# Contributions of seven chunks to the mLSTM states, formed beside the convolution units of the second half

## The chip, the cores and the metric

One core of one Trainium2 chip runs the whole program. The metric is device time in microseconds (us) for one execution. The engines are TensorE (PE), VectorE (DVE), ScalarE (ACT), GpSimd (POOL) and SyncE (SP). Each has its own queue of instructions and goes through it in order, and an instruction waits until what it needs is there. SP and ACT also issue the DMAs.

## What is computed

A transformer block over 2048 rows of width 1024: a norm, one input projection, a pooling mixer and a bidirectional mLSTM scan beside it, an output projection, and a gated MLP. Cut to what matters here:

```python
def mlstm_bidir(q, k, v, gates, st_f, st_b):      # forward scan, and one over the flipped rows
    ...
c_new = decay[..., None, None] * c0 + jnp.einsum('bhs,bhsv,bhsd->bhvd', wk, vc, kc)
n_new = decay[..., None] * n0 + jnp.einsum('bhs,bhsd->bhd', wk, kc)
...
hx_m, _, _ = mlstm_bidir(qx, kx, vx, gx, st_f, st_b)
...
mix_x = jnp.concatenate([pool_x, mlstm_output(hx_m, ox, head_norm[l])], axis=-1) @ w_out[l]
x = x + g1 * mix_x
x = x + g2 * swiglu(modulate(rmsnorm(x, norm2[l]), sh2, sc2), w_up[l], w_down[l])
```

The einsum over the rows of a chunk (weighted keys times values) needs no state. Only the scan, decay times old state plus this contribution, goes from chunk to chunk.

## The kernel before

The sequence is cut into 16 chunks of 128 rows (NCH = 16), the context into 2. The input projection runs in two halves of 1024 rows and by units of two times 128 columns. One unit is seven products of 12 matmuls with 512 columns each (`product`, three matmuls of split operands for each of four k); `unit` numbers them by their operands, A[0] to A[6], and takes them in the order 0, 1, 4, 3, 5, 2, 6. The operands A[0] and A[1] may take buffers named "vt" (four of them, in the pool `vtp`), the others "wh" and "wl".

In the second half come two pool units, the k unit and the q unit (`conv_unit`: after its products each row goes through three steps of the short convolution, a silu, and a store to `s_k` or `s_q`, the "y" instructions at L471 to L474), and then two o units whose products are interleaved. Beside the o units runs `chunk_step`, called in the middle and at the end of each of their products, 18 times in all for 2 context and 16 sequence chunks:

- `load_ahead` and `dma_kv` (L897, L899) load a chunk's keys and values from DRAM on SP;
- `delta_a` turns the keys (two PE transposes, L945) and scales them with the gates (VectorE, L948);
- `delta_b` multiplies with the values (four PE matmuls, L958, eight rows in the profile) and ScalarE copies the result into the state tiles (four copies, L963), which `ST(k)` finds in three tiles, h0, h1 and h5;
- `scan_step` (four VectorE operations, L968) adds decay times the state before. It is called only when both directions' contributions of a step are there, which the order 0, 15, 1, 14, ... gives.

With the o units done, the remaining `chunk_step`s follow one behind another. Then `load_wo` loads the output projection's weights (in small tiles L988 and in big ones L984), scales them (L990, L993) and splits them (L148, L151); its first parts are called among the steps. Then a loop over the chunks: `ml_a` (scores L1090, exponentials L1097, L1099), `ml_b` (L1114, L1120, reciprocal L1125 to L1127, heads L1131 to L1134, L1136), `prep` (transposes L1155), `proj` (L1171 to L1173). The MLP follows.

The order in which each engine meets its instructions is not the order of the code: a scheduler of the framework, with its own model of durations, places them, and an `issue_after` in the code adds an edge to it. The exponentials of all chunks but the first, and the loads of `prep`, have such an edge behind the last copies of the state contributions:

```python
with tc.issue_after(last_act[0].ins), tc.issue_after((copies[-1] if n else last_act[0]).ins):
    for d in range(2):
        for h in range(4):
            nc.scalar.activation(X[:, d, h, :], X[:, d, h, :], AF.Exp, bias=tokq[:, 0, d, h, cc:cc + 1])
```

Of the kernel before, what the change touches and what calls it, by code (L numbers as in the profile page):

```python
# [8 lines left out]
F32 = mybir.dt.float32  # L9
# [12 lines left out]
def tile_hybrid_block(ctx: ExitStack, tc: tile.TileContext, x, c, cx, c_ctx, w_ada, b_ada, norm1, w_in, conv_qk,  # L22
                      gate_bias, pool_w, pool_scale, head_norm, w_out, norm2, w_up, w_down, norm_f, out):
    nc = tc.nc
# [101 lines left out]
    s_g = dram.tile([4, D], F32, name="s_g")  # L126
    s_w = dram.tile([6, 4, 2, P, 512], F32, name="s_w")
    s_e = dram.tile([NCH // 2, P, 512], F32, name="s_e")

# [563 lines left out]
    def run_units(units, psp, wp, tmp, fetch, bg=None):  # L695


        for n, (srcs, sink, after, w, half) in enumerate(units):
            if half:
                make = operands(load_raws(srcs, kept=True), [wp], kept=s_w[w])  # L700
            else:
                make = operands(load_raws(srcs), [wp], keep_=s_w[w])
            A = {}
            for j, i in enumerate(ORDER):
                A[i] = make(i)
                if n == 0 and Btile[j] is None:
                    fetch(j)
            for j, _ in enumerate(unit(A, psp, tmp, sink)):
                if bg and (n, j) in bg:
                    bg.pop((n, j))()  # L710
            after()
# [15 lines left out]
    def conv_unit(bp, half, i0):  # L727
        pre = [bp.tile([P, TH + 3], F32, name=f"pre{r}") for r in range(2)]
        for r in range(2):
            if half == 0:  # L730
                nc.gpsimd.memset(pre[r][:, 1:2], 0.0)
            else:
                nc.gpsimd.tensor_copy(pre[r][:, 0:2], edge[:, i0 + r])
                nc.gpsimd.memset(pre[r][:, TH + 2:TH + 3], 0.0)

        def sink(r, n, ps, sb):
            o = pre[r][:, 2 + n * 512:2 + (n + 1) * 512]
            if sb is None:
                nc.scalar.copy(o, ps)
            else:  # L740
                nc.vector.tensor_tensor(o, ps, sb, op=ALU.add)

        def after():
            for r in (0, 1):
                i = i0 + r
                rows = (s_q, s_k)[i // 2][i % 2 * P:(i % 2 + 1) * P]
                y = bp.tile([P, TH + 1], F32, name="y", bufs=2)
                if half == 0:
                    nc.gpsimd.tensor_copy(edge[:, i], pre[r][:, TH:TH + 2])
                    n, o, t0 = TH - 1, 1, 0  # L750
                else:
                    n, o, t0 = TH + 1, 0, TH - 1
                conv_silu(y[:, :n], pre[r][:, o:], n, conv_w(i), y[:, :n])
                nc.sync.dma_start(rows[:, t0:t0 + n], y[:, :n])
        return in_cols(O_Q + i0 * P), sink, after, i0 // 2, half
# [70 lines left out]
    def o_unit(tmp, half, i0):  # L826
# [8 lines left out]
            nc.scalar.dma_start(s_so[i * P:(i + 1) * P, b * 512:(b + 1) * 512], so)  # L835
        return in_cols(O_O + i0 * P), sink, lambda: None, 4 + i0 // 2, half

    for half in range(2):
        if half:
            Btile = [None] * 7  # L840
# [39 lines left out]
        else:  # L880
# [1 line left out]
            plp.close()  # L882
            rxp = pf.enter_context(pool("rx", 1, "right"))
            with pool("cvp", 1) as bp:
                run_units([conv_unit(bp, half, i0) for i0 in (2, 0)], pu_, wp, tmp, fetch, {(0, 3): fin})
            padr.close()
    tpp.close()

# [17 lines left out]
    bp = pj.enter_context(pool("pja", 1))  # L906
    tmps = (tmp, bp)

    seq = [(True, cc) for cc in range(NCC)] + [(False, cc) for i in range(NCH // 2) for cc in (i, NCH - 1 - i)]
    todo_kv, loaded = list(seq), []  # L910

    def load_ahead():
        if todo_kv:
            is_ctx, cc = todo_kv.pop(0)
            src = (s_kc, s_vc) if is_ctx else (s_k, s_v)
            kp = bp if not is_ctx and len(todo_kv) < 12 and len(todo_kv) % 4 < 2 else kvp
            loaded.append(dma_kv(kp, *src, cc, 2, kvp if is_ctx or cc in (0, NCH - 1) else None))

    for _ in range(2):
        load_ahead()  # L920
# [645 lines left out]
```

## Time and profile before

| | us |
|---|---|
| median of three runs | 2118.39 |
| runs | 2116.07 to 2119.63 |
| profiled execution, its time | 2117.76 |
| its span, first to last instruction | 2115.9 |
| PE busy | 2015.6 (95% of the span) |
| mean granted clock of PE | 0.982 |

The profile is of one execution; 1.9 us of its time lie outside the span. A row of a timeline begins with its start and its length, and ends with the idle time ahead of it and what ended that. "x8" puts equal neighbours together. A DMA's row is its issue, not its landing.

### The profile page before, as it was taken

The page shows a single profiled execution, that of the slowest core. Times are in us where ns is not written, and L with a number is a line of the kernel's source. Part 1 is how long each engine was busy: PE and PEld are TensorE (multiplying, and loading weights), DVE is VectorE, ACT ScalarE, POOL GpSimd, SP SyncE. Part 2 cuts the span into 40 slices and gives each one's busy share as a digit, 9 for nine tenths or more (in the row PEclk, how much of TensorE's full clock was granted, in tenths as well). Part 3 has the DMA queues.
Part 4 walks back from the last instruction along what each step waited for, and adds up shares of the span by engine and source line. Part 5 has one row for each costly group of instructions (what it writes and reads, how often), then busy time and mean ns, then how long its engine had stood idle before and what let it go on. Part 6 is the DMA issues. An engine that isn't in the chain of part 4 may idle for free.

```text
span 2115.9 us, 27589 instructions
## 1 busy us (share of the span) xinstructions
PE 2015.6 (95%) x9482; PEld 1637.0 (77%) x9482; DVE 1365.8 (65%) x2333; ACT 899.1 (42%) x1787; POOL 227.0 (11%) x222
## 2 busy tenths in 40 slices
PE   7999989996999998999999999999999999999998
PEld 3997757775777776788888877888888788888887
DVE  6866868757455566666675588677677554447664
ACT  6643644456444444433333354333333343433442
POOL 1000013211333320000000000000000002004121
PEclk9999999997999999999999999999999999999999
DMA  8598989689586756433342367555565584644642
GB/s 281 169 297 270 301 269 329 219 262 254 138 253 209 241 184 183 140 124 125 100 159 85 100 217 256 189 194 189 174 199 192 190 309 149 226 139 168 226 158 100
DMA packets 365812, 421.42 MB, mean 199 GB/s; under 512 B 23924, under 2 KB 241624, under 8 KB 364904
## 3 DMA queue, kind: packets, MB, share of 16 engines
q1 hardware_dynamic: 319728, 348.22, 50.9%
q10 hardware_dynamic: 45944, 71.43, 10.5%
q8 instruction: 75, 1.23, 0.2%
q14 instruction: 65, 0.53, 0.1%
HBM read 280.45 MB, written 139.12 MB: 198 GB/s over the span
## 4 chain that ended last, share of the span: by engine, by line
PE 74%; DMA 11%; DVE 5%; ACT 4%; issue 3%; SPq 1%; POOL 1%; ACTq 0%; DVEq 0%; POOLq 0%
PE pa L642 8%; PE pa L644 8%; PE pa L643 8%; PE pdn L1392 7%; PE pdn L1393 7%; PE pdn L1394 7%; PE pg L642 4%; PE pg L643 4%; PE pg L644 4%; PE pb L642 2%; PE pb L644 2%; PE pb L643 2%; PE pm L1171 2%; PE pm L1173 2%; PE pm L1172 2%
## 5 line engine op out<-in xcount | busy, mean ns | idle before, releaser
L642 PE MATMUL pa<-h,wh 128*128 128x512 f32 x680 | 271.0, 400 | 7.6 <-ACT p L656 4.7
L644 PE MATMUL pa<-h,wl 128*128 128x512 f32 x680 | 269.8, 397 | 0.3 <-DMA wl<-s_w 0.3
L643 PE MATMUL pa<-h,wh 128*128 128x512 f32 x680 | 269.5, 397 | 0.0
L148 ACT CAST wh<-ws 128x512 fp32r<-128x512 f32 x200 | 123.5, 619 | 281.3 <-PE pg L643 154.2
L1392 PE MATMUL pdn<-ow,op 128*128 128x512 f32 x616 | 236.8, 389 | 1.0 <-ACT op L148 1.0
L1393 PE MATMUL pdn<-ow,op 128*128 128x512 f32 x616 | 237.5, 389 | 0.0
L1394 PE MATMUL pdn<-ow,op 128*128 128x512 f32 x616 | 237.5, 389 | 0.0
L151 DVE TENSOR_TENSOR op<-ra,op 128x512 fp32r<-128x512 f32 x154 | 121.6, 796 | 159.4 <-ACT op L148 159.3
L148 ACT CAST op<-ra 128x512 fp32r<-128x512 f32 x154 | 95.2, 621 | 225.9 <-PE pdn L1394 223.9
L642 PE MATMUL pg<-h,wh 128*128 128x512 f32 x448 | 177.8, 397 | 2.9 <-ACT h L148 1.7
L643 PE MATMUL pg<-h,wh 128*128 128x512 f32 x448 | 178.6, 399 | 0.9 <-DVE h L151 0.8
L644 PE MATMUL pg<-h,wl 128*128 128x512 f32 x448 | 177.5, 396 | 0.0
L151 DVE TENSOR_TENSOR wl<-ws,wh 128x512 fp32r<-128x512 f32 x200 | 136.4, 685 | 55.4 <-ACT wh L148 55.2
L642 PEld LDWEIGHTS pa<-h,wh 128*128 128x128 f32 x680 | 129.0, 190 | 43.2 <-ACT p L656 6.0
L644 PEld LDWEIGHTS pa<-h,wl 128*128 128x128 f32 x680 | 128.5, 189 | 31.1 <-issue 0.5
L643 PEld LDWEIGHTS pa<-h,wh 128*128 128x128 f32 x680 | 128.8, 189 | 30.2 <-issue 1.0
L1424 POOL TENSOR_TENSOR hr<-hr,o 128x1024 f32<-128x1024 f32 x8 | 21.7, 2734 | 1096.7 <-ACT o L1437 927.0
L1392 PEld LDWEIGHTS pdn<-ow,op 128*128 128x128 f32 x616 | 115.6, 188 | 25.5 <-ACT op L148 1.4
L1393 PEld LDWEIGHTS pdn<-ow,op 128*128 128x128 f32 x616 | 115.7, 188 | 23.9
L1394 PEld LDWEIGHTS pdn<-ow,op 128*128 128x128 f32 x616 | 115.7, 188 | 23.9
L613 DVE TENSOR_TENSOR ws<-raw 128x512 f32<-128x512 f32 x100 | 69.0, 690 | 96.3 <-DMA raw<-in_w_up_dram 92.0
L148 ACT CAST vt<-raw 128x512 fp32r<-128x512 f32 x112 | 69.2, 619 | 96.0 <-PE pb L643 41.2
(357 smaller groups left out, 4330.5 us busy)
## 6 DMA issues: line engine op xcount, KB each, us to landing
raw<-in_w_up_dram SPq DMA_DIRECT2D x88, 512.0 KB
ra<-s_act SPq DMA_DIRECT2D x66, 512.0 KB
s_act<-adaw SPq DMA_DIRECT2D x84, 256.0 KB
rwt<-s_t SPq DMA_DIRECT2D x77, 256.0 KB
adaw<-in_w_ada_dram SPq DMA_DIRECT2D x64, 256.0 KB
s_act<-g SPq DMA_DIRECT2D x63, 256.0 KB
s_hb<-hb SPq DMA_DIRECT2D x7, 1792.0 KB
hst<-s_hb ACTq DMA_DIRECT2D x48, 256.0 KB
```

Source lines behind the costliest of these rows:

```text
L148: nc.scalar.copy(hi, src)
L151: eng_lo.tensor_tensor(lo, src, r32(hi), op=ALU.subtract)
L613: nc.vector.tensor_tensor(t, a, b, op=op)
L642: nc.tensor.matmul(ps, lhsT=ah[:, k], rhs=B[:, 0, k], start=st, stop=False, **kw)
L643: nc.tensor.matmul(ps, lhsT=ah[:, k], rhs=B[:, 1, k], start=False, stop=False, **kw)
L644: mm_last[0] = nc.tensor.matmul(ps, lhsT=al[:, k], rhs=B[:, 0, k], start=False, stop=(k == 3), **kw)
L1171: nc.tensor.matmul(pt, lhsT=mh[:, k], rhs=w[:, 0, k % 4], start=(k == 0), stop=False)
L1172: nc.tensor.matmul(pt, lhsT=mh[:, k], rhs=w[:, 1, k % 4], start=False, stop=False)
L1173: nc.tensor.matmul(pt, lhsT=mlo[:, k], rhs=w[:, 0, k % 4], start=False, stop=(k == 7))
L1392: nc.tensor.matmul(ps, lhsT=A[:, 0, ts_], rhs=W[:, 0], start=start, stop=False)
L1393: nc.tensor.matmul(ps, lhsT=A[:, 0, ts_], rhs=W[:, 1], start=False, stop=False)
L1394: nc.tensor.matmul(ps, lhsT=A[:, 1, ts_], rhs=W[:, 0], start=False, stop=stop)
```

## The change

A new function `early_states` forms the contributions of the first seven sequence chunks (0 to 6, NE = 7) during the second half's k and q units: called after products 0, 2, 4, 6 of the k unit and 0, 2, 4, 5 of the q unit, each call turns one chunk and multiplies the one before. Keys of four chunks have room in one tile ("rawx"), values in the three "hst" buffers, the scaled keys in "ws", the result in one of the four "vt" tiles (two copies of 128x258), and from there it is stored to a new DRAM tensor `s_d`. The transposes go to the one bank named "gps", the products to the two named "tp". `chunk_step` is left with 11 chunks: the two of the context, then 15 down to 9, then 7 and 8. When the keys of chunk 15 - e are loaded, `s_d[e]` is read back into the two halves of the state tiles (13 loads).

```diff
+    NE = NCH // 2 - 1
+    s_d = dram.tile([NE, P, 516], F32, name="s_d")
...
+    def early_states(room):
+
+
+        todo_e, got, begun = list(range(NE)), [], []
+
+        def load():
+            if todo_e:
+                cc = todo_e.pop(0)
+                kT = room[:, cc % 4]
+                nc.sync.dma_start(kT, s_k[:, cc * P:(cc + 1) * P].rearrange("(t p) c -> p t c", p=P))
+                vt = wp.tile([P, 4, 129], F32, name="hst", bufs=3)
+                nc.sync.dma_start(vt.rearrange("p h v -> p (h v)"), s_v[cc * P:(cc + 1) * P, :])
+                got.append((cc, kT, vt))
+
+        def estep():
+            new = None
+            if got:
+                cc, kT, vt = got.pop(0)
+                pk = gps.tile([P, 512], F32, name="gps")
+                for p_ in range(2):
+                    nc.tensor.transpose(out=pk[:, p_ * P:(p_ + 1) * P], in_=kT[:, p_, :], identity=ident)
+                kw = wp.tile([P, 4, 2, 64], F32, name="ws", bufs=3)
+                nc.vector.tensor_tensor(
+                    kw, pk[:, 0:256].rearrange("p (h d) -> p h d", h=4)[:, :, None, :].to_broadcast([P, 4, 2, 64]),
+                    tokq[:, 1, :, :, cc].rearrange("p d h -> p h d")[:, :, :, None].to_broadcast([P, 4, 2, 64]),
+                    op=ALU.mult)
+                new = (cc, kw, vt)
+            if begun:
+                cc, kw, vt = begun.pop(0)
+                pds = [tp.tile([P, 512], F32, name="tp") for _ in range(2)]
+                for h in range(4):
+                    hh = h % 2 * 129
+                    nc.tensor.matmul(pds[h // 2][:, hh:hh + 129], lhsT=kw[:, h].rearrange("p d c -> p (d c)"),
+                                     rhs=vt[:, h, :], start=True, stop=True)
+                dt = vtp.tile([P, 4, 129], F32, name="vt").rearrange("p h v -> p (h v)")
+                for p_ in range(2):
+                    nc.scalar.copy(dt[:, 258 * p_:258 * p_ + 258], pds[p_][:, 0:258])
+                nc.sync.dma_start(s_d[cc], dt)
+            if new:
+                begun.append(new)
+            load()
+        for _ in range(2):
+            load()
+        return estep
...
-                run_units([conv_unit(bp, half, i0) for i0 in (2, 0)], pu_, wp, tmp, fetch, {(0, 3): fin})
+                estep = early_states(rxp.tile([P, 4, 2, P], F32, name="rawx"))
+                bg = {(n, j): estep for n, js in enumerate(((0, 2, 4, 6), (0, 2, 4, 5))) for j in js}
+                bg[0, 3] = fin
+                run_units([conv_unit(bp, half, i0) for i0 in (2, 0)], pu_, wp, tmp, fetch, bg)
...
-    seq = [(True, cc) for cc in range(NCC)] + [(False, cc) for i in range(NCH // 2) for cc in (i, NCH - 1 - i)]
+
+    seq = [(True, cc) for cc in range(NCC)] + [(False, cc) for cc in range(NCH - 1, NCH // 2, -1)]
+    seq += [(False, NE), (False, NCH // 2)]
...
-            kp = bp if not is_ctx and len(todo_kv) < 12 and len(todo_kv) % 4 < 2 else kvp
-            loaded.append(dma_kv(kp, *src, cc, 2, kvp if is_ctx or cc in (0, NCH - 1) else None))
+            kp = bp if not is_ctx and len(todo_kv) < 5 and len(todo_kv) % 4 < 2 else kvp
+            loaded.append(dma_kv(kp, *src, cc, 2, kvp if is_ctx or cc >= NCH - 2 else None))
+            e = NCH - 1 - cc
+            if not is_ctx and e < NE:
+                nc.sync.dma_start(ST(e + 1)[0:64].rearrange("p h v -> p (h v)"), s_d[e, 0:64])
+                if e:
+                    nc.sync.dma_start(ST(NCH - e)[64:128].rearrange("p h v -> p (h v)"), s_d[e, 64:128])
```

Where the scheduler puts this, at three places. On PE in the q unit, before: the end of its product A[3] (h_3650) and the beginning of A[1] (h_3622, from "vt"):

```order
L643 MATMUL pg<-h_3650,wh 128x512
L644 MATMUL pg<-h_3650,wl 128x512
L642 MATMUL pg<-h_3650,wh 128x512
L643 MATMUL pg<-h_3650,wh 128x512
L644 MATMUL pg<-h_3650,wl 128x512
L642 MATMUL pb<-h_3622,vt 128x512
L643 MATMUL pb<-h_3622,vt 128x512
L644 MATMUL pb<-h_3622,vt 128x512
```

and after, from the end of its product A[2] (h_3693) to the beginning of A[0] (h_3616, from "vt"):

```order
L647 MATMUL pg<-h_3693,wl 128x512
L861 MATMUL gps<-ident,rawx 128x128 x2
L873 MATMUL tp<-hst,ws 128x129 x4
L547 MATMUL tp<-adaw,onr 128x512
L548 MATMUL tp<-adaw,onr 128x512
L861 MATMUL gps<-ident,rawx 128x128 x2
L873 MATMUL tp<-hst,ws 128x129 x4
L861 MATMUL gps<-ident,rawx 128x128 x2
L873 MATMUL tp<-hst,ws 128x129 x4
L861 MATMUL gps<-ident,rawx 128x128 x2
L873 MATMUL tp<-hst,ws 128x129 x2
L645 MATMUL pa<-h_3616,vt 128x512
```

Before, q's A[0], A[3] and A[1] come ahead of k's A[6]; after, A[3], k's A[6] and A[2] come first, then four chunks of early work, and only then A[0] and A[1].

On SP at the same place, after: the o units' raw load stands ahead of the early keys (rawx), and the stores of k (y) and of the early results (vt) stand among them:

```order
L694 DMA raw<-in_w_in_dram 128x4x128
L850 DMA rawx<-s_k 128x2x128 x4
L757 DMA s_k<-y 128x1025
L850 DMA rawx<-s_k 128x2x128 x2
L852 DMA hst<-s_v 128x516
L878 DMA s_d<-vt 128x516
L850 DMA rawx<-s_k 128x2x128
```

and before, from the raw load for the o units to the store of k:

```order
L691 DMA rawx<-in_w_in_dram 128x4x128
L897 DMA kT<-s_kc 128x2x128
L899 DMA vta<-s_vc 128x516
L897 DMA kT<-s_kc 128x2x128
L899 DMA vta<-s_vc 128x516
L691 DMA raw<-in_w_in_dram 128x8x128
L899 DMA vt<-s_v 128x516 x2
L754 DMA s_k<-y 128x1025
```

The context's loads (s_kc, s_vc) moved behind the early ones.

On ScalarE behind the o units, before: the last state copies (pd) with the casts of w_out (big), up to the second chunk's exponentials:

```order
L148 CAST h_5291<-big 128x512
L963 COPY h_4459<-pd 64x258
L963 COPY h_4458<-pd 64x258
L963 COPY h_4459<-pd 64x258
L963 COPY h_4458<-pd 64x258 x2
L963 COPY h_4459<-pd 64x258
L1143 DMA so<-s_so 128x4x128
L963 COPY h_4458<-pd 64x258
L963 COPY h_4459<-pd 64x258
L1097 ACTIVATE raw<-raw,tokq 128x128 x8
```

and after:

```order
L1021 COPY h_4586<-pd 64x258
L151 CAST h_5238<-big 128x512
L1021 COPY h_4586<-pd 64x258
L1021 COPY h_4587<-pd 64x258
L151 CAST h_5238<-big 128x512
L1201 DMA so<-s_so 128x4x128
L1021 COPY h_4586<-pd 64x258
L1021 COPY h_4587<-pd 64x258
L1155 ACTIVATE raw<-raw,tokq 128x128 x8
L151 CAST h_5238<-big 128x512 x2
L1036 DMA big<-s_g 128x512
```

The second chunk's exponentials came behind both pairs of w_out tiles (h_5228 and the first half of h_5291); they now stand between the casts of the first pair.

## Rows read from the trace of the kernel before

**Rows 1.** The page: busy time of PE, and the chain by engine.

```profile
PE 2015.6 (95%) x9482; PEld 1637.0 (77%) x9482; DVE 1365.8 (65%) x2333; ACT 899.1 (42%) x1787; POOL 227.0 (11%) x222
...
PE 74%; DMA 11%; DVE 5%; ACT 4%; issue 3%; SPq 1%; POOL 1%; ACTq 0%; DVEq 0%; POOLq 0%
```

**Rows 2.** Windows of 50 us: busy time by engine, clock, DMA share.

```profile
core 0: us, PE busy (x) PEld busy (x) DVE busy (x) ACT busy (x) POOL busy (x), PEclk, DMA share, GB/s
...
400.00:450.00 50.00, 48.24 (x235) 39.46 (x234) 28.28 (x40) 27.09 (x45) 6.84 (x12) 1.00 0.84 267
450.00:500.00 50.00, 37.66 (x184) 30.93 (x182) 29.18 (x58) 30.71 (x70) 3.90 (x2) 0.83 0.86 226
500.00:550.00 50.00, 36.81 (x190) 29.95 (x192) 34.28 (x76) 24.32 (x76) 13.90 (x10) 0.86 0.74 212
```

**Rows 3.** Timeline of PE from the o units' end to the projection loop.

```profile
469.52 0.40 PE L644 MATMUL pa<-h,wl 128*128 128x512 f32 x1
...
478.37 4.04 PE L958 MATMUL pd<-vt,kw 128*128 128x129 f32 x16 [4.02 <-ACT h L963]
...
488.47 2.05 PE L958 MATMUL pd<-vt,kw 128*128 128x129 f32 x8
...
496.37 0.38 PE L945 MATMUL gps<-ident,kT 128*128 128x128 f32 x2
...
505.99 1.05 PE L958 MATMUL pd<-vt,kw 128*128 128x129 f32 x8
...
518.21 0.63 PE L1172 MATMUL pm<-h,mh 128*128 128x512 f32 x1
518.64 0.63 PE L1173 MATMUL pm<-h,mlo 128*128 128x512 f32 x1
...
534.43 0.66 PE L1155 MATMUL pm<-ident,h 128*128 128x128 f32 x4
```

**Rows 4.** Timelines of PE, VectorE and ScalarE where the k unit ends.

```profile
404.41 0.50 PE L642 MATMUL pb<-h,vt 128*128 128x512 f32 x1 [1.48 <-DVE pre L741]
...
407.29 0.40 PE L642 MATMUL pa<-h,wh 128*128 128x512 f32 x1
...
403.66 0.69 DVE L741 TENSOR_TENSOR pre<-pb,p 128x512 f32<-128x512 f32 x1 [3.04 <-DMA s_pm<-pd]
404.27 0.68 DVE L741 TENSOR_TENSOR pre<-pa,p 128x512 f32<-128x512 f32 x1
...
407.07 1.29 DVE L472 SCALAR_TENSOR_TENSOR y<-pre,vecs,y 128x1025 f32<-128x1025 f32 x1 [0.85 <-ACT y L471]
408.47 1.29 DVE L473 SCALAR_TENSOR_TENSOR y<-pre,vecs,y 128x1025 f32<-128x1025 f32 x1
...
411.94 1.15 ACT L471 ACTIVATE y<-pre,vecs 128x1025 f32<-128x1025 f32 x1
```

**Rows 5.** Timelines of ScalarE's DMA issues and of VectorE behind the o units.

```profile
476.98 0.68 ACTq L984 DMA_DIRECT2D big<-in_w_out_dram  x1
...
492.22 0.38 ACTq L984 DMA_DIRECT2D big<-in_w_out_dram  x1
...
484.85 1.30 DVE L993 TENSOR_TENSOR big<-big 128x512 f32<-128x512 f32 x2 [3.33 <-DMA big<-in_w_out_dram]
...
499.45 2.42 DVE L990 SCALAR_TENSOR_TENSOR big<-big,vecs 128x512 f32<-128x512 f32 x2 [1.96 <-DMA big<-in_w_out_dram]
...
505.31 0.68 DVE L151 TENSOR_TENSOR h<-big,h 128x512 fp32r<-128x512 f32 x1
...
506.58 1.21 DVE L1099 TENSOR_TENSOR raw<-raw,pqk 128x1024 f32<-128x1024 f32 x1
...
514.12 1.14 DVE L968 SCALAR_TENSOR_TENSOR h<-h,decx 128x129 f32<-128x129 f32 x4
...
529.48 0.35 DVE L1132 SCALAR_TENSOR_TENSOR h<-po,rr,hf 128x128 f32<-128x128 f32 x1 [0.72 <-ACT hf L1131]
```

**Rows 6.** Windows of 5 us, columns as in rows 2.

```profile
475.00:480.00 5.00, 1.63 (x6) 1.37 (x7) 1.07 (x4) 4.79 (x14) 0.00 (x0) 0.50 0.64 128
...
515.00:520.00 5.00, 4.65 (x13) 3.40 (x14) 5.00 (x13) 0.62 (x1) 1.28 (x1) 0.66 1.05 342
```

## The prediction

> **What bounds the kernel now.** I read the page first: TensorE (PE) is busy for 95% of the span and carries 74% of the chain that ended last [rows 1], so a gain can only come from where PE stands still. The table in stretches of 50 us shows where that is: 48.2 of 50 us busy before 450 us, then 37.7 and 36.8 [rows 2]. The timeline of PE shows why. The last 512-wide matmul of the o units starts at 469.52 us and ends at E = 469.9; what follows are the contributions of eleven chunks, in short bursts behind other engines (one stop of 4.02 us behind ScalarE's copies), the first projection, and at S = 534.43 the first transposes of a finished head [rows 3]. Behind S the order of PE through the whole projection loop is the same before and after the change, product for product, so the time moves by what S moves. From E to S are 64.5 us.
>
> **What the change moves ahead of E.** Seven chunks' contributions now run inside the k and q units. Two terms move E.
>
> First, the q unit's start. Its operands A[0] and A[1] lie in the four "vt" buffers, and now the early result tiles take these buffers too. In PE's order the q unit's products A[0] and A[1] therefore stand behind the early work, and k's A[6] and q's A[2] ahead of it. Before, when k's A[6] starts at 407.29 [rows 4], q has three products done. After, when q's A[0] starts, k is complete and q has two done: the same count of products. So the delay of everything behind is the start of q's A[0] minus 407.29, and I walk to it:
> - PE has nothing left at about 399.6: it reaches its stop of before (1.48 us, ending at 404.41, so from 402.9) twelve matmuls and a pair for a gate row earlier, 14 x 0.24 = 3.3 us. k's A[6] waits for VectorE's second L741 to free its bank: start 404.27, 0.68 long, so 404.95; the first of these waited for the last s_pm store, which nothing here moves [rows 4].
> - Twelve matmuls from 404.97 at some 0.24 us each (404.41 to 407.29 holds twelve) and nine of A[2] bring PE to 410; the key transposes of chunk 0 follow (0.38 us a chunk [rows 3]). Their keys are loaded in time: on SP they stand behind the raw load of the o units, which waits for a split on VectorE that now comes ahead of L741, so at about 401.
> - Now a chain of single buffers. There is one bank for the transposes, and VectorE's scaling of chunk 0 lies behind the y steps (407.07 and 408.47, 1.29 us each [rows 4]) and a split: 411.2. Chunk 0's four delta matmuls take 1.05 us [rows 3]. Its copies stand on ScalarE behind y of the second row (L471, which ran from 411.94 for 1.15 us [rows 4], here until 412.5). VectorE's next y waits for the same L471, so chunk 1's scaling ends at 414.5; the second bank, the silu and the rest give 417, 417.9 and 418.3 for the following steps. The cast for A[0] follows on ScalarE at 418.9, and PE starts q's A[0] at 419.2.
> Delay: 419.2 - 407.3 = 11.9 us, with five chunks' transposes and three and a half chunks' deltas done inside it.
>
> Second, the rest of the early work: 3.5 x 1.05 + 2 x 0.38 = 4.4 us. It fills PE between E's products, where before there were no gaps; PE has as many ordinary deltas (seven chunks) ahead of E as it had.
>
> That is E at 469.9 + 11.9 + 4.4 = 486.2. Two costs are not in the trace of before at this place. One is the clock: PE's idle 5 us at 400 us and the sparse work after it resemble the stretches behind E, where the granted clock fell to 0.50 and 0.66, six matmuls in a row stand 0.43 us apart (two rows shown) and eight rows of deltas take 2.05 us instead of 1.05 [rows 3, 6]. If k's A[6] runs so, it costs 12 x 0.19 = 2.3 us, half of it hidden by VectorE's y steps; below nothing it can't go, as the clock is at its full level there today. The other is the DMA queue: seven stores of 264 KB, thirteen loads of 132 KB and the moved loads come into stretches whose engines are busy for 0.84 and 0.86 already [rows 2]; the weight halves read back behind them on SP have some 3 us of room by my walk. Both together 0 to 6 us; I take 2, nearest to the half-hidden A[6]. E' = 488.2, which is 18.3 us later.
>
> The Trainium skill ("TensorE: Matmul & The Clock Gate", section "HAM oscillation — how this bites in real kernels") says that gaps between groups of matmuls send the array back to its cold clock, so that each group begins cold, and advises arranging the work so that PE is not left waiting. By the rows this happened at 475 us and not after the 1.48 us stop; by the page alone the change opens a second such place, which is the second rival below.
>
> **What it takes away behind E.** Of eleven chunks four remain. Their PE work is not the gain: seven times 1.43 us of matmuls and transposes is 10 us, but the stops between them are more. What then comes last is the loading of w_out and VectorE's queue behind it:
> - The first big w_out loads come out of ScalarE's queue after the last small ones, the two sigmoids and the table load, all of which still hang on E: E + 7.1 (476.98), used at 484.85, 7.9 us later [rows 5]. In these 8 us the loads of seven more chunks ran; I take 2 us off, so E' + 13.0.
> - From there VectorE goes through to the last L1132 of the first chunk: four L993 (two in 1.30), four L990 (a pair took 2.42 beside GpSimd; 3.8 for four), nine L151 at 0.6 net, 32 scan operations at 1.14 for four less overlap, three L1099 at 1.21, and small ones: 2.6 + 3.8 + 5.4 + 8.5 + 3.4 + 1.5 = 25.2 us [rows 5]. The second pair of w_out loads is issued after VectorE's split at E' + 17.4 and took 7.2 us before (492.22 to 499.45); VectorE has work until E' + 24, so it hides to within 1 us.
> - ScalarE between the last two L1132 1.1 us, and from the start of the last L1132 to the transposes 4.95 us (529.48 to 534.43) [rows 3, 5].
> Sum: E' + 13.0 + 25.2 + 1.1 + 4.95 = E' + 44.2. The second and third chunk's exponentials no longer wait for the copies of eleven chunks, so they are not late here; ScalarE's copies were one thing that VectorE's scan waited for, and the same scan operations now meet their inputs, of which thirteen half tiles come from DRAM well ahead of E'.
>
> So S' = 488.2 + 44.2 = 532.4, 2.0 us earlier than 534.43. On the profiled execution's own time, 2117.76, that gives **2115.7 us** (the median of the runs shown is 0.6 us above it). A measurement here can tell about 0.2%, or 4.2 us, from no change; the forecast lies inside that.
>
> **Rivals.**
> - *The tail is cheaper.* If w_out lands 5 us after its issue and not 5.9, and VectorE's scans ahead of E' are done so early that half of the 32 behind it run in the waits, S' is E' + 36: 8 us less, about 2107.5. For it: PE's stop of 4.02 us behind ScalarE's copies [rows 3] was for work that now lies ahead of E. Against it: VectorE's order puts the reciprocal of the first chunk behind the second w_out pair.
> - *PE runs cold in the clump* (slower). From 400 to 419 PE has gaps and small matmuls; at half clock the 3.5 chunks inside the chain cost 1.0 more each and five transposes 0.26 each, the products on either side 2.3 each: 3.5 + 1.3 + 4.6 = 9.4 us, less the 2 already counted. S' is then 5.4 later than today: about 2123. It decides from the point at which q's A[0] starts after 422; late weight halves on a full DMA queue would add to it. For it: the clock at 475 us. Against it: VectorE's y steps, not PE, pace most of that chain.
> - *The change does not shorten the tail*, since w_out's loads pace it as they do today: S' = E' + 50, some 2121.5. Against it: before, E to the first use of w_out was only 15 of the 64.5 us.
>
> **How the numbers follow.** Forecast 0.42, cheaper tail 0.25, cold clump 0.25, w_out as today 0.08. The cold clump alone lies mostly beyond +4.2 us, the cheaper tail wholly beyond -4.2; a quarter of the forecast's own spread (5 us to either side, from the 0 to 6 of E' and the landing of w_out) reaches below 2114.2. Faster 0.25 + 0.11 = 0.36, slower 0.20 + 0.05 = 0.25 with some of w_out, same 0.39. Range: from 2107 to 2126, both rivals' times with 3 us beyond the slower one for the DMA queue.
>
> **What would show it.** In the profile after: PE's stop at 400 us of about 5 us instead of 1.5; q's A[0] near 419; the o units' last product near 488; the first big w_out use 13 us later; the transposes near 532, and the same distance from there to the end. I am wrong if q's A[0] starts before 414 or after 424, if PE stops between 420 and 488 for a weight half or a store that holds a "vt" buffer, or if the tail from the last product to the transposes is outside 38 to 50 us.

## The result and the profile after

The changed kernel takes 2131.8 us (median of four runs, 2129.8 to 2135.9) beside 2119.0 us for the kernel before on the same chip: a ratio of 1.0063, 95% interval 1.0046 to 1.0080. A second series gave 2130.0 us and 1.0072 (1.0048 to 1.0096). So the change costs 13 to 14 us, where the forecast was a gain of 2 with a range up to 2126. The forecast was wrong.

The first profiled execution of the changed kernel took 2135.9 us. Its page, lines that answer to [rows 1]: as much PE time as before, and more of the chain in DMA.

```profile
PE 2018.5 (95%) x9482; PEld 1637.3 (77%) x9482; DVE 1367.0 (64%) x2333; ACT 893.0 (42%) x1775; POOL 227.5 (11%) x222
...
PE 72%; DMA 13%; DVE 7%; issue 3%; ACT 3%; SPq 1%; POOL 1%; ACTq 0%; DVEq 0%; POOLq 0%
```

Its windows of 50 us, columns as in [rows 2]:

```profile
400.00:450.00 50.00, 43.30 (x214) 34.31 (x213) 24.27 (x32) 22.73 (x40) 6.90 (x10) 0.97 0.72 231
450.00:500.00 50.00, 42.33 (x217) 34.85 (x215) 28.14 (x58) 25.27 (x49) 3.37 (x3) 0.99 0.91 278
500.00:550.00 50.00, 31.38 (x143) 24.80 (x144) 37.44 (x78) 25.22 (x75) 10.74 (x7) 0.67 0.97 251
```

PE is 5 us less busy between 400 and 450, 5 us more between 450 and 500, and behind that it stands still more than before: 31.4 of 50 us busy where it was 36.8. The last column but one is the point: the DMA engines are busy for 0.97 of the last stretch, before for 0.74.

That execution was 4.4 us late already at 357 us, ahead of the change. The timeline of PE is therefore shown from a second profile (2128.9 us), only 0.3 us late there. It has the end of the k unit, the clump, the o units' last product, the stops of the tail, and the first transposes:

```profile
404.21 0.80 PE L645 MATMUL pa<-h,wh 128*128 128x512 f32 x1 [3.55 <-DVE pre L744]
...
410.56 0.38 PE L861 MATMUL gps<-ident,rawx 128*128 128x128 f32 x2
...
420.83 0.48 PE L645 MATMUL pa<-h,vt 128*128 128x512 f32 x1
...
466.47 0.50 PE L647 MATMUL pg<-h,wl 128*128 128x512 f32 x1 [1.51 <-DMA wl<-s_w]
...
491.50 0.39 PE L647 MATMUL pa<-h,wl 128*128 128x512 f32 x1
...
499.64 2.04 PE L1148 MATMUL pqk<-h,kT 128*128 128x256 f32 x4 [4.83 <-DMA kT<-s_k]
...
519.09 2.05 PE L1148 MATMUL pqk<-h,kT 128*128 128x256 f32 x4 [6.01 <-DMA h<-s_q]
...
528.99 1.10 PE L1148 MATMUL pqk<-h,kT 128*128 128x256 f32 x4 [3.97 <-DMA h<-s_q]
...
542.61 0.66 PE L1213 MATMUL pm<-ident,h 128*128 128x128 f32 x4
```

So E' = 491.9 and S' = 542.6: the tail is 50.7 us, in the first profile 53.3, and the forecast had 44.2. On ScalarE the same tail holds the big w_out loads (L1042) and the loads of `prep` (L1204; the row with CAST is ScalarE's split of pmx):

```profile
500.82 0.54 ACTq L1042 DMA_DIRECT2D big<-in_w_out_dram  x1
...
512.70 0.41 ACTq L1042 DMA_DIRECT2D big<-in_w_out_dram  x1
...
514.50 0.37 ACTq L1204 DMA_DIRECT2D pmx<-s_pm  x1
...
520.23 0.62 ACT L151 CAST mh<-pmx 128x512 fp32r<-128x512 f32 x1 [3.40 <-DMA pmx<-s_pm]
...
521.11 0.38 ACTq L1042 DMA_DIRECT2D big<-in_w_out_dram  x1
```

and VectorE's rows are the use of the last small w_out load but one, the three uses of the big ones, a split that lies beside GpSimd's work, and the last L1190 of the first chunk:

```profile
495.02 0.75 DVE L1048 SCALAR_TENSOR_TENSOR wos<-wos,vecs,g1r 128x512 f32<-128x512 f32 x1 [1.09 <-DMA wos<-in_w_out_dram]
...
506.77 2.49 DVE L1051 TENSOR_TENSOR big<-big 128x512 f32<-128x512 f32 x4
...
518.79 1.41 DVE L1048 SCALAR_TENSOR_TENSOR big<-big,vecs 128x512 f32<-128x512 f32 x2 [0.41 <-DMA big<-in_w_out_dram]
...
527.70 1.42 DVE L1048 SCALAR_TENSOR_TENSOR big<-big,vecs 128x512 f32<-128x512 f32 x2
...
530.95 2.46 DVE L154 TENSOR_TENSOR h<-big,h 128x512 fp32r<-128x512 f32 x1 [0.15 <-ACT h L151]
...
538.07 0.35 DVE L1190 SCALAR_TENSOR_TENSOR h<-po,rr,hf 128x128 f32<-128x128 f32 x1 [0.72 <-ACT hf L1189]
```

Three things stand out. The third w_out load is issued 8.4 us after the second (9.8 in the first profile); before it was 3.3 us (492.22 [rows 5] and 495.51). It stands on ScalarE behind the split of pmx, which waits for a load of its own. The last small w_out load but one is used at E' + 3.1 (E' + 3.6 in the first profile; before, E - 0.1), with everything behind it on ScalarE that much later. And between the first use of the big loads and the last L1190 VectorE is busy nearly all the time: it waits 0.41 us for the second load and next to nothing for the third. So that the third load is late does not show as a wait of VectorE.

Windows from the first use of the big loads to the last L1190, columns as in [rows 2], in the second profile and in the first:

```profile
506.77:538.07 31.30, 13.14 (x65) 9.87 (x64) 28.68 (x60) 17.16 (x50) 8.69 (x5) 0.76 1.08 267
...
507.30:540.23 32.93, 14.97 (x60) 11.05 (x60) 29.77 (x58) 16.76 (x49) 8.49 (x5) 0.63 1.08 257
```

### The profile page after: what moved, and what is told of

Same layout as the page of the kernel before. It is cut to its first block, busy times and chain, and to the rows that moved or that the text cites. A ratio compares the mean times of both kernels' runs of the same rounds, so it can differ in the third digit from the quotient of the medians.

```text
span 2133.8 us, 27567 instructions
## 1 busy us (share of the span) xinstructions
PE 2018.5 (95%) x9482; PEld 1637.3 (77%) x9482; DVE 1367.0 (64%) x2333; ACT 893.0 (42%) x1775; POOL 227.5 (11%) x222
## 4 chain that ended last, share of the span: by engine, by line
PE 72%; DMA 13%; DVE 7%; issue 3%; ACT 3%; SPq 1%; POOL 1%; ACTq 0%; DVEq 0%; POOLq 0%
PE pa L645 7%; PE pa L646 7%; PE pa L647 7%; PE pdn L1450 7%; PE pdn L1451 7%; PE pdn L1452 7%; PE pg L647 4%; PE pg L646 4%; PE pg L645 4%; PE pm L1229 2%; PE pb L645 2%; PE pb L646 2%; PE pb L647 2%; PE pm L1230 2%; PE pm L1231 2%
## 5 line engine op out<-in xcount | busy, mean ns | idle before, releaser
L647 PEld LDWEIGHTS pa<-h,wl 128*128 128x128 f32 x680 | 128.5, 189 | 30.7 <-issue 0.5
L1229 PE MATMUL pm<-h,mh 128*128 128x512 f32 x256 | 107.6, 420 | 1.6 <-DVE hb L300 1.5
```

Source lines behind the costliest of these rows:

```text
L647: mm_last[0] = nc.tensor.matmul(ps, lhsT=al[:, k], rhs=B[:, 0, k], start=False, stop=(k == 3), **kw)
L1229: nc.tensor.matmul(pt, lhsT=mh[:, k], rhs=w[:, 0, k % 4], start=(k == 0), stop=False)
```

## The experiments

PE's order is the same in all kernels up to a matmul at some 357 us, the 1801st of the trace. From there three lengths are counted in each profiled execution: to the end of the o units' last product (E), from E to the first transposes of a finished head (S), and from S to the last matmul. The ratio is that of the timed runs.

| kernel | matmul 1801 to E | E to S | S to the end | time against before |
|---|---|---|---|---|
| before | 112.4 | 64.5 | 1573.7 | 1 |
| before, second profile (e10) | 113.1 | 62.7 | 1577.7 | |
| after | 129.9 | 53.3 | 1581.0 | 1.0063 (1.0046 to 1.0080) |
| after, second profile (e9) | 134.1 | 50.7 | 1576.8 | 1.0072 (1.0048 to 1.0096) |
| e1 tail alone | 114.6 | 50.6 | 1572.3 | 0.9941 (0.9923 to 0.9960) |
| e2 early work alone | 135.1 | 61.8 | 1578.6 | 1.0104 (1.0080 to 1.0127) |
| e3 no reading back | 128.9 | 52.0 | 1576.6 | 1.0030 (1.0014 to 1.0046) |
| e4 q in wh, wl | 140.0 | 45.9 | 1581.3 | 1.0105 (1.0081 to 1.0128) |
| e5 edge of prep | 133.1 | 51.0 | 1576.7 | 1.0050 (1.0031 to 1.0069) |
| e6 later calls | 134.8 | 43.0 | 1585.4 | 1.0083 (1.0056 to 1.0111) |
| e7 e5 and e6 | 135.2 | 46.0 | 1579.7 | 1.0072 (1.0044 to 1.0100) |
| e8 less GpSimd | 132.6 | 54.9 | 1573.3 | 1.0073 (1.0048 to 1.0098) |
| e11 e5 and e8 | 133.3 | 48.7 | 1578.6 | 1.0063 (1.0038 to 1.0087) |
| e12 e5 and e3 | 130.7 | 45.9 | 1577.6 | 1.0012 (0.9999 to 1.0024) |

**The two halves apart.** e1 leaves the early work out and reads rows of the values back in place of its results; e2 does the early work and then all chunks as before.

```diff
-                estep = early_states(rxp.tile([P, 4, 2, P], F32, name="rawx"))
-                bg = {(n, j): estep for n, js in enumerate(((0, 2, 4, 6), (0, 2, 4, 5))) for j in js}
-                bg[0, 3] = fin
+                bg = {(0, 3): fin}
...
-                nc.sync.dma_start(ST(e + 1)[0:64].rearrange("p h v -> p (h v)"), s_d[e, 0:64])
+                nc.sync.dma_start(ST(e + 1)[0:64].rearrange("p h v -> p (h v)"), s_v[e * P:e * P + 64, :])
...
```

> Leaves out the early work (transposes, products, copies, stores of the seven chunks); the thirteen half tiles that come back from DRAM are rows of the values instead, so the output is not the block's. What is left is the short tail with its loads. The changed kernel stands at 2131.8 us, the kernel before at 2119.0. If the error lies ahead of the o units' end (front theory), the tail here is the predicted 44.2 us from the o units' last product to the first transposes, the last product is at 470 as before, and the time is 2119.0 - 20.3 = 2099. If the tail was mis-sized and is paced by its loads whatever stands ahead of it (tail theory), it takes the 53.4 us that the changed kernel's profile shows, and the time is 2119.0 - 11.1 = 2108. If w_out paces it as before, 64 us and 2119.

> The early work of the seven chunks with its stores is done as in the changed kernel, but nothing is read back, and all eighteen chunks are taken in the old order beside and behind the o units, so the early results are not used. Front theory: the last product of the o units moves by 18 to 22 us as in the changed kernel, the tail behind it stays at 64.5 us, and the time is 2119.0 + 18.3 to 22 = 2137 to 2141. Rival (the profile of the changed kernel began the region 4 us late by chance, and the old tail is paced in part by loads that don't wait for the o units' end): the last product moves by 18 or less, the tail shrinks to 58 to 60, and the time is 2131 to 2133, no worse than the changed kernel.

In e1 the o units end at 471.1 and the first transposes are at 521.7, 50.6 us on. Here the third w_out load waits for pmx as it does after:

```profile
491.32 0.43 ACTq L1040 DMA_DIRECT2D big<-in_w_out_dram  x1
...
500.25 0.62 ACT L151 CAST mh<-pmx 128x512 fp32r<-128x512 f32 x1 [3.97 <-DMA pmx<-s_pm]
500.26 0.38 ACTq L1040 DMA_DIRECT2D big<-in_w_out_dram  x1
```

So the short tail is worth 12.5 us (0.0059 of 2117), not the 20.3 of the forecast, with nothing of the early work ahead of it: the tail theory. It has the thirteen loads that read back, too. e2 costs 22 us, the upper end of what was expected; its tail is about as long as before's. A front of 22 and a tail of 12.5 give 9.5; measured are 13 to 14, and no run shows where the other 4 come from.

**Reading back.** e3 drops the thirteen loads:

```diff
-                nc.sync.dma_start(ST(e + 1)[0:64].rearrange("p h v -> p (h v)"), s_d[e, 0:64])
-                if e:
-                    nc.sync.dma_start(ST(NCH - e)[64:128].rearrange("p h v -> p (h v)"), s_d[e, 64:128])
+                pass
...
-            nc.vector.scalar_tensor_tensor(b[:, h], a[:, h], decx[:, h, k:k + 1], b[:, h], op0=ALU.mult, op1=ALU.add)
+            nc.vector.scalar_tensor_tensor(b[:, h], a[:, h], decx[:, h, k:k + 1], a[:, h], op0=ALU.mult, op1=ALU.add)
```

> The changed kernel without the thirteen loads that bring the early contributions back (1.7 MB); the scan adds the old state in place of the contribution, same operations and sizes, so the output is not the block's. Tail theory (the DMA engines are full behind the o units: busy share 0.97, 251 GB/s in 500 to 550 us): 1.7 MB at 251 GB/s are 6.8 us, the first use of the big w_out loads and the second and third of them come earlier, and the time falls by 4 to 7 us to 2125 to 2128. Rival (the loads land well ahead and only fill idle DMA time): 2131.8, no change.

The ratio fell to 1.0030, some 0.0037 or 8 us below the two series of the changed kernel, though the intervals meet at 1.0046. VectorE and ScalarE's queue in e3, where E is 485.6, show what became earlier:

```profile
485.80 0.75 DVE L1046 SCALAR_TENSOR_TENSOR wos<-wos,vecs,g1r 128x512 f32<-128x512 f32 x1 [0.67 <-DMA wos<-in_w_out_dram]
...
491.92 0.55 ACTq L1040 DMA_DIRECT2D big<-in_w_out_dram  x1
```

The last small w_out load but one is used at E + 0.2 instead of E + 3.1 to 3.6, and the first big ones are issued at E + 6.4 instead of E + 8.9 to 9.5. They are used at E + 14.5, though, hardly earlier than after's 14.9 and 15.5; the third load still stands behind pmx, and the tail, 52.0, is no shorter. In this profile the gain lies ahead of E.

**The edge of prep.** In the code, the three loads of `prep` have an edge behind the fourth last copy of the state contributions. With eleven chunks' copies behind E that was late; with four it is early, and the scheduler puts these loads, and the split of pmx, ahead of the third w_out load. e5 ties them to that load:

```diff
-                    nc.scalar.dma_start(st2, w_out[k * P:(k + 2) * P, ns].rearrange("(e p) c -> p e c", e=2))
+                    wo_last[0] = nc.scalar.dma_start(st2, w_out[k * P:(k + 2) * P, ns].rearrange("(e p) c -> p e c", e=2))
...
-        with tc.issue_after(copies[-4].ins):
+        with tc.issue_after(wo_last[0].ins):
```

> The changed kernel; only the edge of the three loads of prep is another: they stand behind the last load of w_out instead of behind the fourth last copy. In the changed kernel the third big w_out load is issued at 523.21, behind ScalarE's cast of pmx, which waits 5.04 us for its load; before, that load is issued 3.3 us after the second. Edge theory: the copies end early now, so the old edge lets the loads of prep past the w_out load; with the new edge the third load is issued as soon as VectorE's splits free its buffer (520.0), 3 us earlier, it lands 3 us earlier, and the tail from the last o product to the transposes shrinks from 53.4 to about 50, the time from 1.0063 of before to 1.005. Rival (VectorE is the bound from 507 us on, and pmx is late now): the tail stays at 53 to 55 and the ratio at 1.0063 or above.

ScalarE's issues in e5:

```profile
512.67 0.43 ACTq L1042 DMA_DIRECT2D big<-in_w_out_dram  x1
...
517.14 0.42 ACTq L1042 DMA_DIRECT2D big<-in_w_out_dram  x1
...
521.12 0.37 ACTq L1204 DMA_DIRECT2D pmx<-s_pm  x1
```

The third load comes 4.5 us after the second instead of 8.4 to 9.8, as the edge theory has it. The ratio, 1.0050, and the tail, 51.0, are too near to after's to tell alone. From the last L1190 to the transposes are 3.5 us, in after 4.5 and 4.9.

**Both.** e12 joins e3 and e5.

> The edge of the fifth run and, as in the third run, nothing read back from DRAM (the scan adds the old state in place of the contribution; the output is not the block's). Load theory: what the forecast missed behind the o units is late loads, of which both changes take some away, the third w_out load behind pmx and 1.7 MB of read-backs; together the tail falls from 50.7 to 53.3 in the two profiles of the changed kernel to 48 to 49, the first transposes are 3 us instead of 7.7 later than before, counted from matmul 1800, and the ratio is 1.001 to 1.003. VectorE theory: the tail is VectorE's own work, so with its operations unchanged the tail stays at 50 to 52 and the ratio at 1.005.

This decides between the two theories. The ratio is 1.0012, its interval clear of both series of the changed kernel. The first transposes come 176.6 us after matmul 1801, where before has 176.9 and 175.8, and the tail is 45.9 us, below the 48 to 49 that were expected, with VectorE's operations unchanged. It doesn't give each part its share: against e5, from which e12 differs by the reading back alone, the intervals lie apart (to 1.0024, from 1.0031); against e3, from which it differs by the edge alone, they overlap (to 1.0024, from 1.0014). So the cost of the reading back is shown, and that of the edge only together with it. Rows of VectorE, ScalarE and PE in e12, where E is 491.0:

```profile
491.16 0.75 DVE L1046 SCALAR_TENSOR_TENSOR wos<-wos,vecs,g1r 128x512 f32<-128x512 f32 x1 [0.37 <-DMA wos<-in_w_out_dram]
...
497.53 0.49 ACTq L1040 DMA_DIRECT2D big<-in_w_out_dram  x1
...
510.28 0.37 ACTq L1040 DMA_DIRECT2D big<-in_w_out_dram  x1
...
515.71 0.37 ACTq L1040 DMA_DIRECT2D big<-in_w_out_dram  x1
...
536.90 0.66 PE L1211 MATMUL pm<-ident,h 128*128 128x128 f32 x4
```

What reading back does is seen on SP. In the second profile of after, seven of the thirteen loads that read back, the last at 463.62, are issued ahead of the first small w_out loads, at E' - 25.7:

```profile
463.62 0.45 SPq L973 DMA_DIRECT2D h<-s_d  x1
...
466.16 2.03 SPq L1046 DMA_DIRECT2D wos<-in_w_out_dram  x2
```

In e12 the same small loads are issued at E - 30.7:

```profile
460.26 1.28 SPq L1044 DMA_DIRECT2D wos<-in_w_out_dram  x2
```

**VectorE beside GpSimd.** e8 leaves GpSimd's product of wb and qd out for four chunks (`if n > 3:` ahead of it), e11 joins it with the edge of e5.

> The changed kernel without GpSimd's product of wb and qd for the first four chunks of the projection loop (wb alone is used, so the output is not the block's); the order of the other engines is the same. Between 507 and 540 us VectorE's operations that lie beside GpSimd's take longer (four scans 2.15 for 1.13, a split 2.74 for 0.68, and others: 5.8 us in all, 2.7 beside the products left out). Contention theory: these 2.7 us come off the tail, 53.4 to 50.7, and the ratio falls to about 1.005. Rival: VectorE then waits for w_out's loads instead, and the tail stays within 1 us of 53.4.

> The edge of the fifth run and the missing GpSimd products of the eighth together (the output is not the block's). Co-bound theory: behind the first use of w_out VectorE's work beside GpSimd and the second and third w_out loads end nearly together, so that each change alone gives little (2.3 us, and -1.6); together they give the sum of both savings, 2.9 + 2.7 us, and the tail is 47 to 49 instead of 53.4. Rival (the loads of w_out alone bind, at the pace at which full DMA engines land them): the tail is 50 to 52, no shorter than with the edge alone.

In e8 VectorE is busy 27.3 us from the first use of w_out to the last L1191 (in after 29.8 and 28.7) and waits 5.6 us (3.2 and 2.6), most of it for the second w_out load, so the stretch, 32.9 us, is no shorter:

```profile
526.41 1.41 DVE L1048 SCALAR_TENSOR_TENSOR big<-big,vecs 128x512 f32<-128x512 f32 x2 [2.69 <-DMA big<-in_w_out_dram]
```

So taking the contention away did not shorten the tail: 54.9, 1.5 above the 53.4 of the first profile, where the rival had said within 1. e11 has a tail of 48.7, inside the 47 to 49 of the co-bound theory, but counted from the first use of w_out to S it has 35.2 us and e5 alone 34.7. Its shorter tail comes from an earlier first use (E + 13.5), for which the runs give no cause. Its ratio, 1.0063, shows no gain, and the co-bound theory isn't shown. But e11 shows what VectorE's work is by itself. The stretch from the first use to the last L1191, in e11 and in e12:

```profile
506.67:538.37 31.70, 16.18 (x68) 11.48 (x67) 24.57 (x59) 17.20 (x50) 4.27 (x2) 0.66 1.02 260
...
503.15:533.41 30.26, 15.67 (x68) 11.18 (x67) 26.26 (x59) 17.08 (x50) 8.69 (x5) 0.70 1.06 273
```

VectorE is busy 24.6 us in e11, with the same operations, and waits 7.1: for loads, and for ScalarE. Either way the stretch is over 30 us.

**The early work elsewhere.** e4 gives q's A[0] and A[1] other buffers, so that they needn't stand behind the early results; e6 puts the calls behind k's last product and q's seven, e7 adds the edge.

```diff
-                make = operands(load_raws(srcs, kept=True), [wp], kept=s_w[w])
+                make = operands(load_raws(srcs, kept=True), [wp], early=0 if w == 0 else 2, kept=s_w[w])
```

```diff
-                bg = {(n, j): estep for n, js in enumerate(((0, 2, 4, 6), (0, 2, 4, 5))) for j in js}
+                bg = {(n, j): estep for n, js in enumerate(((6,), range(7))) for j in js}
```

> The changed kernel, but the q unit's operands A[0] and A[1] take the buffers of its other operands (wh, wl) and not the four vt buffers, which the early results keep for themselves. Front theory: q's A[0] need not stand behind the early work, which then costs little more than its own PE time, 7 x 1.43 = 10 us instead of 18 to 22; the last product of the o units is at 480 to 482 and the time 2131.8 - 8 = 2124. Rival: the stops come from the single bank for transposes and from the scaling behind VectorE's y steps wherever the early work stands, so that the last product stays at 488 to 492 and the time at 2131.8; or the operands in wh and wl are late themselves, and it is slower than 2132.

> The changed kernel, but the eight calls of the early work come after the k unit's last product and the seven products of the q unit, so that q's A[0] and A[1] take their vt buffers ahead of the early results, and PE meets one chunk's early work per product instead of five in a row. Clump theory: of the 16.4 us by which the stretch from the last pool matmul to the last o product is longer than before (88.8 for 72.4), 10 are PE time of the early work and 6 are stops in the row of early work; these go, the stretch is 82 to 84, and the ratio falls from 1.0063 to about 1.0035. Rival: the stops come back elsewhere in the q unit and the o units (keys and values that land late, the s_d stores and reads still under way at the o units' end), the stretch stays at 87 or more, and the ratio at 1.006 or above.

> The edge of the fifth run and the calls of the sixth together. If the two theories hold and add up: stretch 83, tail 50, the transposes 9 us earlier than in the changed kernel against the last pool matmul, a ratio of 1.002: still no faster than before. If either falls, the ratio is that of the other alone.

In e4 the front theory fell: it is 22 us slower than before. The last case of its rival came about, in part at least, as the first of these three stops of PE is for a half in wh; the other two are for the keys:

```profile
404.45 0.50 PE L645 MATMUL pg<-h,wh 128*128 128x512 f32 x1 [1.76 <-DMA wh<-s_w]
...
439.07 0.44 PE L1003 MATMUL pb<-ident,kT 128*128 128x128 f32 x2 [2.30 <-DMA kT<-s_kc]
...
452.31 0.67 PE L1003 MATMUL pb<-ident,kT 128*128 128x128 f32 x2 [3.81 <-DMA kT<-s_k]
```

In e6 the row of early work is gone from PE's order, but the clump theory fell: the stretch ahead of E did not shrink (134.8 us from matmul 1801, in after 129.9 and 134.1), and the ratio is 1.0083, as the rival had it. The first transposes still come 177.7 us after matmul 1801, 6 to 7 us earlier than after; that gain is in the tail. Some 10 us are lost in the projection loop: PE's order there is another from the 17th matmul behind S on, and from the first chunk's transposes to the last chunk's it is 283.3 us (535.36 to 818.68), where the eleven profiles with before's loop order have 268.6 to 273.7. e4 is like it: a tail of 45.9 and a loop of 277.1. Between the first use of w_out and the last L1190 VectorE has 33 operations in e6 and 31 in e4, where it has 58 in after, so their short tails say nothing of the loads: part of the work stands behind S. That it is what makes the loop longer would fit, and isn't shown. e7 is no better than e5.

**Once more the same.**

> The changed kernel once more, unchanged, beside the kernel before on the same chip: to see what of its profile is chance. In the first profile it is 4.4 us late before the change begins (instruction 1800 of the matmuls, 361.9 for 357.5), 6.4 us more at the first transposes, and 7.3 us more from there to the end, where the order through the loop is the same. If the last part belongs to the change, it is there again with 5 to 9 us and the ratio is again 1.006; if it is chance, the part behind the transposes lies within 4 us of before's 1573.7 and the ratio at 1.003 to 1.005.

> The kernel before once more, for a second profile. The first has 112.4 us from instruction 1800 to the last o product, 64.5 to the first transposes, 1573.7 from there to the end. If single profiles can be compared, each is within 2 us of that; if chance is as large as in the profiles of the variants (1572 to 1577 behind the transposes for those with the same order), the last one differs by up to 4.

Behind S the two profiles of before have 1573.7 and 1577.7, those of after 1581.0 and 1576.8: single profiles scatter by 4 us there, and the 7.3 us of the first comparison are no measure of the change. The ratio did not fall with it, as the expectation had tied to it. From matmul 1801 to S the pairs are 176.9 and 175.8 against 183.3 and 184.8, which is 7.7 us. The timed runs say 13 to 14. The rest, some 6 us, lies outside that stretch and has no cause yet: in the means of the pairs it is 2.9 us ahead of matmul 1801 and 3.2 us behind S. The profiles of kernels with the early work reach matmul 1801 at 356.3 to 363.2 us, those without it at 356.4 to 357.5, in the same order of PE, and chance and a cause can't be told apart with so few.

No version beat the kernel before; e12, which comes level with it, leaves out part of the work.

## Why the prediction was wrong

The steps of the forecast against the two profiles of after. Where a step moves, the means of two profiles on either side are compared, counted from matmul 1801:

| step | forecast | measured |
|---|---|---|
| k's A[6] starts | 404.27 | 404.21 |
| q's A[0] starts | 419.2 | 420.83 |
| E moves by | 18.3 | 19.3 |
| E' to the first big w_out use | 13.0 | 15.5, 14.9 |
| from there to the last L1190 | 26.3 | 32.9, 31.3 |
| last L1190 to the transposes | 4.95 | 4.9, 4.5 |
| tail | 44.2 | 53.3, 50.7 |
| S moves by | -2.0 | 7.7 |
| the time moves by | -2.0 | 13 to 14 |

(q's A[0] and A[6] are from the second profile, which is 0.3 us late at 357 us; in the first they start at 423.5 and 408.7, 4.4 us late there.)

**The front was right.** From the start of k's A[6] to q's A[0] the walk had 14.9 us; the first profile has 14.8, the second 16.6. PE's stop ahead of it is 3.55 us rather than 5, since PE came to it later; the early work runs in the order that was read, and E moves by 1 us more than was said. The forecast named a stop for a weight half between 420 and 488 as a sign against itself: there is one, 1.51 us at 466.47 (1.33 in the first profile), so the "two costs" were nearer to 3 than to 2.

**The cold clump came in small.** Windows of the second profile, columns as in [rows 2], behind the stop of 3.55 us, in the row of early work, at its end, and behind a later stop of 2.31 us:

```profile
404.00:407.00 3.00, 2.79 (x7) 2.21 (x8) 1.72 (x3) 1.74 (x2) 0.00 (x0) 0.50 0.72 206
410.00:413.00 3.00, 2.92 (x19) 2.11 (x17) 0.69 (x1) 2.90 (x4) 0.00 (x0) 1.00 0.26 101
...
417.00:421.00 4.00, 3.68 (x19) 3.51 (x18) 1.77 (x4) 1.86 (x5) 0.00 (x0) 0.57 0.88 272
441.50:443.00 1.50, 1.44 (x3) 1.16 (x4) 1.20 (x2) 0.27 (x1) 1.48 (x1) 0.50 1.06 375
```

Seven matmuls 0.43 us apart instead of 0.24 cost 1.3 us at 404, which is within the 2 that were counted, and the stretch at half clock from 417 to 421 accounts for about 1.5 of the 1.8 us by which the second profile's walk is longer (the first has 1.00 there). The second rival had put 9.4 us on it. The Trainium skill ("TensorE: Matmul & The Clock Gate", section "HAM oscillation — how this bites in real kernels") says that a group behind a gap starts cold; by the rows at 404 and 441 the trace agrees, at a fraction of the rival's 9.4 us. In the first profile six matmuls behind the same stop of 3.55 us come at the full clock, and only the eight after them stand 0.43 us apart.

**The step that failed is the tail**, 6.5 to 9 us too short. Two of its terms were mis-sized.
- *The first use of w_out, "E' + 13.0"*, measured at 14.9 and 15.5. "I take 2 us off", as fewer loads run, and thirteen half tiles "from DRAM well ahead of E'": the loads that read back come to 1.7 MB that weren't there. They land in time for the scan, but on SP they stand ahead of the small w_out loads, which are used 3 us later after E', and the sigmoid, the table load and the first big loads stand behind these on ScalarE. With the reading back and the old edge away (e12), the first use is at E + 12.2.
- *VectorE's way from there to the last L1190 (L1132 in the kernel before), 25.2 + 1.1 us*, measured at 31.3 and 32.9. The count was right as work (24.6 us busy in e11) and wrong as a bound. Beside GpSimd the same operations take longer (such as 2.46 for 0.68 at 530.95), so VectorE is busy 28.7 and 29.8 us, and it waits 2.6 and 3.2 us. Where GpSimd's product is left out, waits take the place of what is gained, and none of the runs with these operations has under 29.7 us (e1). What would bring the stretch to 26.3 stays open.

"The second pair of w_out loads ... hides to within 1 us" came true of VectorE's wait (0.41 us at most). But it takes the pair as one. ScalarE's order after shows `prep`'s loads and the split of pmx between its two loads; the piece of it that is quoted with the change ends just ahead of them. The second load is issued at E' + 20.8 to 21.6, the third at E' + 29.2 to 31.4. An edge tied to "the fourth last copy" had kept that order right as long as the copies were late. What this costs by itself is within the noise; with the new edge the last step, to the transposes, is 3.5 us instead of 4.5 to 4.9.

Without the reading back and the old edge (e12) the tail is 45.9, near the forecast's 44.2, and in part by luck: 12.2 and 3.5 us at its ends, for 13.0 and 4.95, make up for 30.3 us between, for 26.3.

The third rival, E' + 50 and given 0.08, has the tail's length nearly right. Its reason, that w_out's loads pace the tail, holds for the first use; later VectorE hardly waits for them. Its time, 2121.5, is 10 us short.

**"The time moves by what S moves" did not hold either.** S came 7.7 us later, which alone would make 2125.5 and lie inside the range. The other 6 us have no cause yet. In the timed runs e12 is level with before, so most of them went with the reading back and the edge.

**Even right, it was no gain.** With both away, in e12, which leaves out part of the work, the change is level with before. The tail gives 17.7 us, and the same work ahead of E costs 18: PE was busy for 48.2 of 50 us there [rows 2], so its work and its stops are paid, and behind E PE's time was not what the tail lacked.

## What to carry to other kernels

Work that is moved off a stretch full of waits into one where the engine is busy is paid in full there, while what comes back is only what the stretch's longest chain gives up; find that chain with the moved work already gone. Count an engine's work there at the durations that it has beside its neighbours, as the rows of that stretch show them. An edge or a queue place that was tied to the moved work ("after the last copies") moves with it: read the new order of each queue to the end of the stretch, and ask of each load what waiting instruction now stands ahead of it. Loads that land in time can still be dear, if they stand in a queue ahead of others that don't.

## What the runs showed of the hardware

- Reading back and the old edge add up in the timed runs: 0.0017 for the edge and 0.0037 for the reading back, from the mean 1.0067 of the changed kernel, make 1.0013; measured with both is 1.0012. The 0.0017 alone is not clear of noise. Single profiles of the same stretch scatter by 2 to 4 us, as much as the smaller of the two.
- Shorter operations on VectorE changed nothing where a load came next: in e8 it was busy 1.4 to 2.4 us less than in after, and waited 2.69 us for the second w_out load.
- After the stops of 3.55 and 2.31 us PE's granted clock was 0.50 in the second profile, that is 1.2 of 2.4 GHz, with seven matmuls 0.43 us apart. After the first profile's stop of 3.55 us it was at the full level for six matmuls, and then eight stood 0.43 us apart. After the stop of 1.48 us before [rows 4] and that of 1.51 us at 466.47 the matmuls behind the first stand some 0.23 us apart.
